# The fifth product of three regions, made of seven quarter products onto PSUM instead of one whole product

## The chip, the cores and the metric

The kernel runs on one core of one Trainium2 chip, as one program. The metric is the device time of one execution in microseconds (us), lower is better. A run is a few executions; the time before is the median of three, 1533.28 us (1532.73 to 1537.7). Engines: PE (TensorE) multiplies, DVE (VectorE) and ACT (ScalarE) add and copy, POOL (GpSimd) and SP (SyncE) start DMAs. Matmul results land in PSUM, which has eight banks (tiles named `ps0` to `ps7` here, 128 x 512 fp32 each). Each engine executes its own queue strictly in the order in which the program wrote it and waits where a semaphore tells it to.

## What is computed

```python
m, k, n = 4096, 4096, 4096
x = np.matmul(a, b)                    # fp32 inputs
return np.where(x > 0, x, alpha * x)   # alpha = 0.01
```

## The kernel before

The output is cut into 16 regions of 1024 x 1024, four groups of rows (g) by four columns (j). Region (0, 0) is a plain blocked product. The other 15 are made one after the other, in the order (0,1), (0,2), (0,3), (1,2), (1,0), (1,3), (1,1), (2,2), (2,0), (2,3), (2,1), (3,2), (3,0), (3,1), (3,3), each by one level of Winograd's form of Strassen's product: A's rows of the group and B's columns are each seen as 2 x 2 blocks (512 x 2048 and 2048 x 512), and seven products of such blocks replace eight. The operands are fp16, sums of blocks are made by DVE. The list PRODUCTS gives the order: a11, a12, s2, s3, s1, a22, s4, each with its block of B (s1 to s4 are sums of blocks of A, the blocks of B are turned into sums in place by `b_sum`). Products one, three, five and seven collect in the four banks `y`, the others in the four banks `z`; a whole product is 64 matmuls of 128 x 128 by 128 x 512 (`product`, L807). Region i + 1 swaps the banks of y and z.

In most regions with g > 0 some products are split a second time in the same way: each block is cut into 2 x 2 quarters, and seven quarter products of 16 matmuls with 256 columns (`quarter_product`, L752) replace the eight that 64 matmuls of 512 columns amount to. Before the change these are the fourth product (`fourth_in_quarters`; not in the first region of a group), the sixth (`sixth_in_quarters`) and the seventh (`seventh_in_quarters`, at the very end `seventh_at_the_end`); the sixth and seventh stay whole in the last region of a group if another group follows (`turning`). In what follows, 4.1 to 4.7, 5.1 to 5.7 and 6.1 to 6.7 are the quarter products of the fourth, fifth and sixth product in the order in which PE gets them.

A product in quarters needs, on the side of A, four sums of quarters. They are made once in a group (`sums_of_a`), kept in DRAM (`kept_q`) and brought back by SP's queue (`load_sums`, L744; for the seventh by ACT's queue) into rooms of the pool `a16`. On the side of B it needs one quarter changed in place (`t3_of_b`, L681) and three sums (`sums_of_b`: sum 2 is L687, sum 4 L689, sum 1 L691), made by DVE in every region into rooms of a tile t. Each is one instruction on 128 x 2048 fp16.

How the order around the change is set: all of it is written by hand (`manual_schedule`); there is no planner. Each engine's queue holds its instructions in the order of the program text below. Tiles in a pool with few buffers bring waits: a new PSUM bank waits until the last reader of the old tile in that bank is done. Semaphores for PSUM go by bank: a DVE add on one half of a bank waits for matmuls into the other half of it, if they stand ahead of it in the text, and the reverse.

In a region such as (2,3), DVE's queue from the fourth product on was: `b_sum` on three blocks (L589); the five adds that take the fourth product's banks into the accumulators v (L1131; the first reads the bank called fourth, the second the one called other); `t3_of_b`, `sums_of_b` (2, 4, 1) for the sixth, `t3_of_b` for the seventh; `add_v` (L978), which adds v into the accumulators u2. These ran beside the fourth and fifth product. Then come the sixth's steps, in `sixth_in_quarters`:

```python
quarter_product(x[0, 0], b[0, 0], into(one), True)      # 6.1
add(v[:2], y[:2]); more(0, 0, one); add(v[2:], y[2:])
quarter_product(sx(1), t(1), into(other), True)         # 6.2
more(1, 1, other)
...                                                     # 6.3
leave(v_pairs, 1, 1)                                    # leaky relu, L313
quarter_product(sx(2), t(2), into(one))                 # 6.4
more(0, 1, one)
...                                                     # 6.5: sx(4), b[1, 1], other
quarter_product(sx(3), b[0, 1], into(one))              # 6.6
```

`add` is L973, `more` is L862. 6.4 writes the bank that the first `more` reads, 6.5 that of the second, 6.6 that of the third. In the last region, (3,3), `judge` tests statistics of the inputs on DVE: three reductions after the fourth product (L621) and, behind `add_v`, a chain of twelve small instructions (L630 to L637).

Of the kernel before, what the change touches and what calls it, by code (L numbers as in the profile page):

```python
# [8 lines left out]
P = 128  # L9
DT = mybir.dt.float16  # L10
# [14 lines left out]
KC = 8  # L25
# [23 lines left out]
def kernel(  # L49
# [610 lines left out]
    kept_s2 = dram_pool.tile([2, P, KC * RM], DT, name="kept_s2")  # L660
    kept_q = {name: dram_pool.tile([4, P, QUARTER], DT, name=f"kept_q{name}") for name in ("a22", "s4")}
    kept_s3 = dram_pool.tile([P, QUARTER], DT, name="kept_s3")
# [29 lines left out]

    def sums_of_a(g, name, room):

        x = {key: q.rearrange("p c m e -> p c (m e)") for key, q in quarters_of_a(g, name).items()}
        made = {}

        def make(n, x0, x1, op):
            made[n] = room(n)
            f = lambda t: made[t].rearrange("p (c m) -> p c m", m=2 * HALF) if isinstance(t, int) else x[t]  # L700
            nc.vector.tensor_tensor(f(n), f(x0), f(x1), op)
            nc.sync.dma_start(kept_q[name][n - 1], made[n])

        make(1, (1, 0), (1, 1), ADD)
        make(2, 1, (0, 0), SUB)
        make(3, (0, 0), (1, 0), SUB)
        make(4, (0, 1), 2, SUB)
# [17 lines left out]
    def sums_of_s3(g, some, room=None):  # L725
# [4 lines left out]
        for n in some:  # L730
# [5 lines left out]
            if n == 4:  # L736
                nc.sync.dma_start(kept_s3, room)

    def s3_rooms(g):
# [43 lines left out]
    for i, (g, j) in enumerate(regions):  # L783
# [64 lines left out]

        def sixth_in_quarters(pairs, banks, v_pairs, v, y, tq, sq):

# [21 lines left out]
            quarter_product(sx(1), t(1), into(other), True)  # L872
            more(1, 1, other)
            following(4)
            next_t[2] = tq[1]
# [7 lines left out]
            quarter_product(sx(4), b[1, 1], into(other))  # L883
            following(1, sq[4])
            next_t[4] = tq[2]
            sums_of_b(y7, next_t, (4,))
            more(0, 1, other)
            quarter_product(sx(3), b[0, 1], into(one))
            following(3)
            more(1, 0, one)  # L890
# [134 lines left out]
        in_quarters = g > 0 and not turning  # L1025
        in_fourth = in_quarters and not first_of_group
        second_of_group = in_fourth and regions[i - 2][0] != g
        early = [measure(i, *block) for block in EARLY.get((g, j), [])]
        for m in early[:1]:
            m.begin()  # L1030
        if first_of_group and g:
            keep_s2(g)

        product(0, y, True)
# [82 lines left out]
        if late_ones:  # L1117
            late_ones[0].end()
        if in_quarters and first_of_group:
            sq = {4: t[:, 3]}  # L1120
            sums_of_a(g, "a22", lambda n: sq.setdefault(n, sq[4] if n == 4 else new_a16()))
            keep_x21(g, "a22")

        z = [new_bank(zbank + mt) for mt in range(MT)]
        if in_fourth or turning and g:
            v_pairs, v, parts = fourth_in_quarters(z, tq, {**s3_rooms(g), 4: a_quarter(sx4)})
            if turning:
                for n in range(3):
                    turn_a_in(0, 1, n)
            for to, bank in parts:  # L1130
                nc.vector.tensor_add(to, bank, to)  # L1131
            if turning:
                add_v()
        else:
            product(3, z, True)
            v_pairs, v = keep(z, side)
        if in_fourth:
            sq = {n: t[:, 3] if n == 4 else new_a16() for n in (1, 2, 3, 4)}
            load_sums("a22", sq, (1, 2, 3, 4))
# [17 lines left out]
        if final:  # L1157
            judged = judge(b_pool.tile([1, P * 6], FP32, name="line", tag="b12"))
            next(judged)
        if in_quarters:  # L1160
            t3_of_b(quarters_of_b(i, 1, 0))
            sums_of_b(quarters_of_b(i, 1, 0), tq)
            t3_of_b(quarters_of_b(i, 1, 1))
            add_v()
            if final:
                good = next(judged)

        product(4, y, False)
        if turning:
            new_s(g + 1, "s1")  # L1170
        if in_quarters:
            tq, sq = sixth_in_quarters(u2_pairs, [new_bank(zbank + mt) for mt in range(MT)], v_pairs, v, y, tq, sq)
        else:
# [6 lines left out]
        if fifth:  # L1180
            fifth = measure(i + 1, *fifth)
            fifth.begin()
            fifth.end()
        fetch_b(i + 1, [(0, 0)], ks)

# [113 lines left out]
```

## Time and profile before

| what | value |
|---|---|
| median of three executions | 1533.28 us (1532.73 to 1537.7) |
| the profiled execution | 1536.2 us, of which its span on the core is 1534.2 us |
| PE busy | 1524.3 us, 99% of the span |
| DVE busy | 1158.9 us, 76% |
| ACT busy | 425.5 us, 28% |
| moved by DMA | 351.26 MB by the queues, mean 229 GB/s |
| region (2,3) on PE | 970.18 to 1062.11 us, 91.93 us |
| its fourth, fifth, sixth, seventh product | from 1011.62, 1023.84, 1037.66, 1049.88 us |

The span runs from the first to the last instruction on the core. In the timeline of an engine each line has the start, the duration, the engine, the line of the kernel, the operation with what it writes and reads, the count of instructions merged into the line, and in brackets the idle time ahead of it and what ended it. Matmuls are pipelined, so the time that one takes is read from start to start, not from the duration. A DVE instruction also overlaps the end of the one ahead of it by some 0.09 us, so DVE too is counted from start to start.

### The profile page before, as it was taken

The page shows a single profiled execution, that of the slowest core. Times are in us where ns is not written, and L with a number is a line of the kernel's source. Part 1 is how long each engine was busy: PE and PEld are TensorE (multiplying, and loading weights), DVE is VectorE, ACT ScalarE, POOL GpSimd, SP SyncE. Part 2 cuts the span into 40 slices and gives each one's busy share as a digit, 9 for nine tenths or more (in the row PEclk, how much of TensorE's full clock was granted, in tenths as well). Part 3 has the DMA queues.
Part 4 walks back from the last instruction along what each step waited for, and adds up shares of the span by engine and source line. Part 5 has one row for each costly group of instructions (what it writes and reads, how often), then busy time and mean ns, then how long its engine had stood idle before and what let it go on. Part 6 is the DMA issues. An engine that isn't in the chain of part 4 may idle for free. (4 is left out here: it accounts for less than half of the span.)

```text
span 1534.2 us, 21785 instructions
## 1 busy us (share of the span) xinstructions
PE 1524.3 (99%) x8667; PEld 847.1 (55%) x8667; DVE 1158.9 (76%) x1207; ACT 425.5 (28%) x730; POOL 258.5 (17%) x426
## 2 busy tenths in 40 slices
PE   9999999999999999999999999999999999999998
PEld 4444444444446567574544747557544475746656
DVE  4368867765699686768769698676976987687677
ACT  2201344646310213103641130312464103041210
POOL 5641110143202011022220001010331100101000
PEclk9999999999999999999999999999999999999999
DMA  9999995998879999899797939669899892948723
GB/s 246 186 215 203 237 281 169 180 197 172 231 277 287 258 278 275 251 289 255 170 288 266 321 148 208 260 157 322 166 241 283 235 349 72 294 162 190 301 97 140
DMA packets 192002, 351.26 MB, mean 229 GB/s; under 512 B 18705, under 2 KB 131601, under 8 KB 178834
## 3 DMA queue, kind: packets, MB, share of 16 engines
q0 software_dynamic: 119808, 112.22, 46.2%
q1 hardware_dynamic: 65458, 211.98, 37.0%
q10 hardware_dynamic: 6624, 25.56, 4.4%
q8 instruction: 70, 1.15, 0.3%
q14 instruction: 42, 0.34, 0.1%
HBM read 344.98 MB, written 114.82 MB: 300 GB/s over the span
## 5 line engine op out<-in xcount | busy, mean ns | idle before, releaser
L807 PE MATMUL ps<-b,a 128*128 128x512 f16 x2624 | 571.1, 379 | 0.5 <-DMA b<-in_b_dram 0.3
L807 PE MATMUL ps<-b,s 128*128 128x512 f16 x2240 | 489.2, 379 | 0.0
L807 PEld LDWEIGHTS <-a 128*128 128x128 f16 x2624 | 256.7, 98 | 308.8 <-issue 1.5
L807 PEld LDWEIGHTS <-s 128*128 128x128 f16 x2240 | 219.1, 98 | 262.5 <-issue 0.4
L589 DVE TENSOR_TENSOR b<-b 128x4096 f16<-128x4096 f16 x104 | 234.6, 2286 | 42.7 <-DMA b<-in_b_dram 34.1
L533 POOL DMA_DIRECT2D b<-in_b_dram x128 | 94.9, 746 | 860.1 <-PE ps L752 437.2
L820 ACT COPY c<-ps 128x512 f32<-128x512 f32 x164 | 84.8, 596 | 469.1 <-PE ps L807 433.3
L142 DVE STREAM_TRANSPOSE a<-a 128x512 uint32<-128x512 uint32 (+2 forms) x120 | 127.0, 1106 | 100.8 <-DMA a<-in_a_dram 100.8
L133 POOL DMA_DIRECT2D a<-in_a_dram x252 | 137.6, 554 | 266.8 <-ACT junk L608 98.2
L608 ACT ACTIVATE junk<-a 128x512 bf16<-128x512 f16 x192 | 121.1, 631 | 99.1 <-DMA a<-in_a_dram 93.8
L752 PEld LDWEIGHTS <-q 128*128 128x128 f16 x1424 | 139.3, 98 | 16.7 <-issue 0.6
L313 DVE SCALAR_TENSOR_TENSOR c<-c 128x1024 f32<-128x1024 f32 (+2 forms) x123 | 141.5, 1190 | 3.8 <-ACT c L820 3.5
L973 DVE TENSOR_TENSOR c<-ps,c 128x512 f32<-128x512 f32 x140 | 87.5, 682 | 55.5 <-PE ps L807 41.8
L231 ACT ACTIVATE sq<-b 128x2048 bf16<-128x2048 f16 x64 | 118.3, 1910 | 37.1 <-DVE sq L240 29.4
L752 PEld LDWEIGHTS <-a 128*128 128x128 f16 x1200 | 117.4, 98 | 18.0 <-issue 0.4
L283 PE MATMUL ps<-b,a 128*128 128x512 f16 x512 | 112.4, 379 | 0.6 <-DVE part L324 0.2
L752 PE MATMUL ps<-b,q 128*128 128x256 f16 x784 | 92.0, 273 | 0.4 <-DVE c L862 0.4
L752 PE MATMUL ps<-b,a 128*128 128x256 f16 x752 | 88.3, 273 | 0.0
L283 PEld LDWEIGHTS <-a 128*128 128x128 f16 x512 | 49.7, 98 | 61.2 <-issue 2.1
L909 ACT COPY c<-ps 128x512 f32<-128x512 f32 x9 | 5.3, 586 | 269.7 <-PE ps L752 148.3
L752 PEld LDWEIGHTS <-s 128*128 128x128 f16 x624 | 61.0, 98 | 7.1
L862 DVE TENSOR_TENSOR c<-ps,c 128x512 f32<-128x512 f32 x80 | 52.2, 683 | 14.4 <-PE ps L752 14.4
(104 smaller groups left out, 904.8 us busy)
## 6 DMA issues: line engine op xcount, KB each, us to landing
b<-in_b_dram POOLq DMA_DIRECT2D x136, 512.0 KB, 11.7
out_dram<-c SPq DMA_DIRECT2D x240, 256.0 KB, 6.3
a<-in_a_dram POOLq DMA_DIRECT2D x244, 128.0 KB, 5.8
b<-kept_half SPq DMA_DIRECT2D x28, 1024.0 KB, 10.9
b<-kept SPq DMA_DIRECT2D x20, 1024.0 KB, 9.2
q<-kept_qs ACTq DMA_DIRECT2D x40, 512.0 KB, 7.8
s<-kept_s SPq DMA_DIRECT2D x18, 1024.0 KB, 7.7
q<-kept_qa SPq DMA_DIRECT2D x28, 512.0 KB, 7.3
```

Of the source, the lines that this page charges most:

```text
L133: nc.gpsimd.dma_start(a16[32 * q:32 * q + 32], src.rearrange("(g i) w -> i g w", i=32))
L142: nc.vector.transpose(part.rearrange("p c m e -> p c (m e)").bitcast(U32) .rearrange("p c (g i) -> p g c i", i=32), src[:, :, i * n:(i + 1 ...
L231: nc.scalar.activation(to, self.parts[n], SQUARE)
L283: nc.tensor.matmul(ps, a_cols(at[0, h, u], c, mt, (h, u) == (0, 0)), bt[0, u, nt][:, c, :], start=first, stop=last,)
L313: nc.vector.scalar_tensor_tensor(t, t, alpha, t, op0=MULT, op1=MAX if alpha <= 1 else MIN)
L533: nc.gpsimd.dma_start(t[:, c:c + 4, :], b_rows(j, u, c, 4, nt, g > 0))
L589: nc.vector.tensor_tensor(f(to), f(x0), f(x1), op)
L608: nc.scalar.activation(junk, piece[:, q, :], SQUARE, accum_out=to[:, 4 * n + q:4 * n + q + 1])
L752: nc.tensor.matmul(to[m], xq[:, c // 2, rows, c % 2], yq[:, c, :], start=first and c == 0 and m < banks, stop=c == KC - 1, skip_group_chec ...
L807: nc.tensor.matmul(banks[mt], a_cols(t, c, mt, t is first_a), B(half, nt, k)[:, c, :], start=first and (k, c) == todo[0], stop=(k, c) == t ...
L820: nc.scalar.copy(kept[mt], banks[mt])
L973: nc.vector.tensor_add(to, bank, to)
```

## The change

In the regions (2,3), (3,1) and (3,3) (the set FIFTH) the fifth product (s1 by a block of B) is made by the new `fifth_in_quarters`: seven quarter products. 5.2, 5.3 and 5.5 add straight onto quarters of the banks y. The other four go into two spare banks of z, `one` and `other`; ACT copies each of these from PSUM into a room in SBUF, and DVE adds the room onto the quarters of y that share it, in PSUM (L876 and L897 of the changed kernel). The rooms lie in the quarter of a22 that the later quarter products don't read; what lay there (a sum of quarters of s3, also used by the fourth product) is kept in DRAM as `kept_s31` and brought back in the next region.

Four sums of quarters of s1 are made in (2,0) and (3,0), on DVE beside their fourth product, and kept in DRAM; each region of FIFTH loads them for its fifth product, and the sums of a22 for its sixth only then. On the side of B, `t3_of_b` and `sums_of_b` for the fifth product come ahead of the fourth's five adds on DVE (sum 1 between the second and the third). `add_v` moves to directly behind these adds. The work for the sixth and seventh product that stood beside the whole fifth product is dealt out: `t3_of_b` and sums 2 and 1 between the steps of the fifth; sum 4 and the seventh's `t3_of_b` in the sixth, behind its second `more` and ahead of `leave`. In (3,3) the chain of `judge` moves behind the fifth product's steps. The fetch of the next region's first block of B takes its halves in the other order.

```diff
@@ sums_of_a @@
-    def sums_of_a(g, name, room):
+    def sums_of_a(g, name, room, some=(1, 2, 3, 4), made=None):
 ...
@@ sums_of_s3 @@
             if n == 4:
                 nc.sync.dma_start(kept_s3, room)
+            if n == 1 and g > 1:
+                nc.sync.dma_start(by_chunk(kept_s31), sx[1])
 ...
+        def fifth_in_quarters(y, one, other, tq, sq, between):
+            b = quarters_of_b(i, 0, 0)
+            x = quarters_of_a(g, "s1")
+            t = lambda n: b_quarter(tq[n])
+            sx = lambda n: a_quarter(sq[n])
+            onto = lambda r, n: [y[2 * r + m][:, n * HALF:(n + 1) * HALF] for m in range(2)]
+            rooms = by_chunk(x21(g, "a22")).bitcast(FP32)
+            rooms = [rooms[:, :2], rooms[:, 2:]]
+
+            def copied(bank):
+                rooms.append(rooms.pop(0))
+                nc.scalar.copy(rooms[1], pair(bank))
+                return rooms[1]
+
+            def more(r, n, room):
+                for m, to in enumerate(onto(r, n)):
+                    nc.vector.tensor_add(to, to, room[:, m])
+
+            quarter_product(x[0, 0], b[0, 0], into(one), True)
+            room = copied(one)
+            quarter_product(sx(4), b[1, 1], onto(0, 1))
+            more(0, 0, room)
+            next(between)
+            quarter_product(x[1, 1], t(4), onto(1, 0))
+            quarter_product(sx(2), t(2), into(one))
+            room = copied(one)
+            quarter_product(x[0, 1], b[1, 0], onto(0, 0))
+            more(0, 1, room)
+            next(between)
+            quarter_product(sx(1), t(1), into(other), True)
+            room = copied(other)
+            more(0, 1, room)
+            more(1, 1, room)
+            quarter_product(sx(3), b[0, 1], into(one))
+            room = copied(one)
+            for m in range(2):
+                to = pair(y[2 + m])
+                nc.vector.tensor_add(to, to, room[:, m].unsqueeze(1).to_broadcast([P, 2, HALF]))
@@ sixth_in_quarters @@
             quarter_product(sx(1), t(1), into(other), True)
             more(1, 1, other)
+            if between:
+                next(between)
             following(4)
 ...
             quarter_product(sx(4), b[1, 1], into(other))
-            following(1, sq[4])
+            following(1, None if between else sq[4])
 ...
             quarter_product(sx(3), b[0, 1], into(one))
-            following(3)
+            following(3, sq[3] if between else None)
@@ the loop over the regions @@
+        if i and regions[i - 1] in FIFTH:
+            for c in range(KC // 2):
+                nc.sync.dma_start(by_chunk(x21(g, "a22"))[:, c], by_chunk(kept_s31)[:, c])
 ...
+        s1_sums = {}
+        if s1_here:
+            sums_of_a(g, "s1", lambda n: t[:, n - 1], (1, 2, 3), s1_sums)
+        if in_fifth:
+            t5 = {2: t[:, 0], 4: t[:, 1], 1: t[:, 2]}
+            t3_of_b(quarters_of_b(i, 0, 0))
+            sums_of_b(quarters_of_b(i, 0, 0), t5, (2, 4))
 ...
-            for to, bank in parts:
+            for n, (to, bank) in enumerate(parts):
+                if in_fifth and n == 2:
+                    sums_of_b(quarters_of_b(i, 0, 0), t5, (1,))
                 nc.vector.tensor_add(to, bank, to)
-            if turning:
+            if turning or in_fifth:
                 add_v()
 ...
+        if s1_here:
+            sums_of_a(g, "s1", lambda n: t[:, 3], (4,), s1_sums)
+        if in_fifth:
+            s5 = {n: t[:, 3] if n == 3 else new_a16() for n in (4, 2, 1, 3)}
+            load_sums("s1", s5, (4, 2, 1, 3))
+        elif in_fourth:
 ...
+        def for_the_sixth():
+            y6 = quarters_of_b(i, 1, 0)
+            t3_of_b(y6)
+            yield
+            sums_of_b(y6, tq, (2, 1))
+            yield
+            sums_of_b(y6, tq, (4,))
+            t3_of_b(quarters_of_b(i, 1, 1))
+            yield
 ...
+        if in_fifth:
+            fifth_in_quarters(y, new_bank(zbank + 3), new_bank(zbank + 1), t5, s5, between)
+            sq = {n: t[:, 3] if n == 3 else new_a16() for n in (1, 2, 4, 3)}
+            load_sums("a22", sq, (1, 2, 4, 3))
             if final:
                 good = next(judged)
-
-        product(4, y, False)
+        else:
+            product(4, y, False)
 ...
-        fetch_b(i + 1, [(0, 0)], ks)
+        fetch_b(i + 1, [(0, 0)], (1, 0) if in_fifth else ks)
```

## The prediction

> **What bounds the kernel now.** I read the page's parts 1 and 2 first, then PE's timeline, then who kept PE waiting, then DVE's timeline beside the products that the change touches.
>
> ```profile
> span 1534.2 us, 21785 instructions
> PE 1524.3 (99%) x8667; PEld 847.1 (55%) x8667; DVE 1158.9 (76%) x1207; ACT 425.5 (28%) x730; POOL 258.5 (17%) x426
> PEclk9999999999999999999999999999999999999999
> ```
>
> PE is the bound, at full clock. So the change is worth what it takes from PE's queue, less each wait that it puts there. The waits of PE, and PE's rows in region (2,3), products four to seven:
>
> ```profile
> PE ps L752 <- DVE c L862: 0.4, 1, 0.4
> ...
> 1022.10 1.91 PE L752 MATMUL ps<-b,a 128*128 128x256 f16 x16
> 1023.84 13.98 PE L807 MATMUL ps<-b,s 128*128 128x512 f16 x64
> 1037.66 1.91 PE L752 MATMUL ps<-b,a 128*128 128x256 f16 x16
> ...
> 1049.88 3.66 PE L752 MATMUL ps<-b,s 128*128 128x256 f16 x32
> ```
>
> A whole product takes 1037.66 - 1023.84 = 13.82 us, seven quarter products 1049.88 - 1037.66 = 12.22 us, 1.747 us each. PE stands still there at no time. DVE in the same place:
>
> ```profile
> 1019.57 0.69 DVE L1131 TENSOR_TENSOR c<-ps,c 128x512 f32<-128x512 f32 x1
> 1021.17 0.69 DVE L1131 TENSOR_TENSOR c<-ps,c 128x512 f32<-128x512 f32 x1 [0.92 <-ACT c L840]
> 1022.91 0.69 DVE L1131 TENSOR_TENSOR c<-ps,c 128x512 f32<-128x512 f32 x1 [1.05 <-ACT c L842]
> 1024.04 1.29 DVE L1131 TENSOR_TENSOR c<-ps,c 128x512 f32<-128x512 f32 x2 [0.44 <-PE ps L752]
> 1025.25 1.21 DVE L681 TENSOR_TENSOR b<-b 128x2048 f16<-128x2048 f16 x1
> 1026.50 1.23 DVE L687 TENSOR_TENSOR q<-b 128x2048 f16<-128x2048 f16 x1
> ...
> 1037.21 1.29 DVE L973 TENSOR_TENSOR c<-ps,c 128x512 f32<-128x512 f32 x2 [3.69 <-PE ps L807]
> 1039.60 0.69 DVE L862 TENSOR_TENSOR c<-ps,c 128x512 f32<-128x512 f32 x1 [1.11 <-PE ps L752]
> ...
> 1042.01 2.35 DVE L313 SCALAR_TENSOR_TENSOR c<-c 128x1024 f32<-128x1024 f32 x2
> 1044.84 0.69 DVE L862 TENSOR_TENSOR c<-ps,c 128x512 f32<-128x512 f32 x1 [0.49 <-PE ps L752]
> ```
>
> From the fourth product's adds to the sixth's third `more` (1044.84) DVE idles only 0.92 + 1.05 + 0.44 + 3.69 + 1.11 + 0.49 = 7.7 us. What happens when it is late there, region (1,2) shows: the third `more`, directly behind L313, ends at 489.41, and 6.6, due at 487.10 + 1.75 = 488.85, starts at 489.46.
>
> ```profile
> 487.10 1.91 PE L752 MATMUL ps<-b,q 128*128 128x256 f16 x16
> 489.46 1.91 PE L752 MATMUL ps<-b,q 128*128 128x256 f16 x16 [0.45 <-DVE c L862]
> ...
> 486.46 2.35 DVE L313 SCALAR_TENSOR_TENSOR c<-c 128x1024 f32<-128x1024 f32 x2
> 488.73 0.68 DVE L862 TENSOR_TENSOR c<-ps,c 128x512 f32<-128x512 f32 x1
> ...
> 1519.47 0.74 DVE L938 TENSOR_TENSOR c<-ps,c 128x256 f32<-128x256 f32 x2
> ```
>
> **The change, part by part.** *PE.* 13.82 - 12.22 = 1.59 us less in each of three regions, 4.8 us in all: the most that there is to win, 0.31%.
>
> *Prices on DVE*, start to start: 128 x 2048 fp16 sum 1.14 us (1.26 where it reads what the one ahead wrote), 128 x 512 add from PSUM 0.605 (four rows of L862 in 2.48), L313 and L978 2.27 a pair. The adds back into PSUM (eight of 128 x 256, two of 128 x 512 a region) are in no row of before. Nearest is L938, 128 x 256 from PSUM into SBUF: two end in 0.74, so 0.33 each; I take that, and 0.605 for the wide ones. Lower end: nothing (an added instruction gives no gain). Upper end: double, 0.69 and 1.21.
>
> [...]
>
> *The queue of DVE in (2,3), moved along.* New ahead of the first L1131: `t3_of_b` and sums 2 and 4, each reading the one before, 3 x 1.25 = 3.76, so it starts at 1023.33 and ends at 1024.03. It frees the bank into which 5.1 goes, due at 1023.84: PE starts at 1024.08, **0.24 late**. Then one add, sum 1, three adds, `add_v` (0.605 + 1.14 + 1.82 + 2.27): 1029.77. First pair of adds into PSUM: 1030.43, in time for 5.5 at 1031.06 (0.6 to spare). `t3_of_b`: 1031.57. The next pair stands behind 5.5 (same banks), which ends at 1032.81; with 0.2 from PE to DVE it runs to 1033.67: here DVE idles 1.4 us although it is behind. Sums 2 and 1: 1036.07. Four adds: 1037.39. Two wide ones: 1038.60 (their copy by ACT is there at 1037.14). The fifth product ends at 1024.08 + 12.23 = 1036.31.
>
> Sixth: two L973, `more`, two L973, `more` (2 x 1.82): 1042.23; 6.4 and 6.5, due at 1041.55 and 1043.30, are served (first `more` 1040.41). Then, new and ahead of `leave`: sum 4 and the seventh's `t3_of_b`, 2.28, then L313 2.27: 1046.78. Only now the third `more`, whose end at 1047.47 releases 6.6 at 1047.52. 6.6 was due at 1036.31 + 5 x 1.747 = 1045.04: **2.49 late** (0.01 from rounding). Region: -1.59 + 0.24 + 2.49 = **+1.14**. Region (3,1) has the same rows at the same distances (b_sum ends 7.95 us after its fourth product starts in both): **+1.14**.
>
> *(3,3)* is the same but for `judge`: its chain ran beside the fifth product from 1499.08 to 1502.27, now 3.25 us stand between the fifth's last adds and the sixth's first. Its three reductions (0.27) fall into the 1.4 us idle. First `more` 3.25 later: 6.4 waits 2.26, 6.5 another 0.07, 6.6 another 3.41: -1.59 + 0.24 + 5.74 = **+4.39**.
>
> *The seventh product* then starts as late as the sixth ended; DVE leaves the sixth about 5 us after that start (4.3 before) and has 6.42 us idle later there, so the lateness dies in it.
>
> *ACT.* Four copies of 0.59 a region; it idled from 1022.9 to 1053.6 apart from four DMA issues. 5.4 needs the copy of 5.1, done 0.83 after 5.1's end, 2.7 ahead of 5.4. Nothing, as long as ACT is free within these 2.7 us; beyond, 5.4 would be late by the rest.
>
> *(2,0) and (3,0).* Four sums of s1, 4.7 us of DVE, against 3.69 idle ahead of L973 at 945.27 and 1.1 in smaller gaps: nothing on PE. On SP the store of the fourth sum now stands ahead of the four loads for the sixth: in (2,0) they leave at about 937.3 and not at 925.16. 6.2 (947.5) is 10 us away; loads of `kept_qa` land in 3.1 to 8.7. The last load waits for that store too (stores of such sums: median 2.6 to 7.0): 937.3 + 7.0 + 8.7 = 953.0 against 6.5 at 952.7, so 0 to 0.3; I take 0.
>
> *Other DMAs in the three regions.* The loads for the fifth leave where the sixth's did (1017.05, then every 1.75); even at 8.7 they land at 1025.8, 1027.5, 1029.2, 1031.0, needed at 1025.8, 1029.3, 1032.8, 1034.6. The sixth's leave as 5.2, 5.4, 5.6, 5.7 end: at 8.7 they land at 1036.3, 1039.8, 1043.3, 1045.0, needed at 1038.1, 1041.6, 1043.3, 1045.0. No wait, but no room. SP stands with the last of these until 5.7 ends; behind it are only the stores of `leave`, due 10 us later. POOL's fetches of the next region's first block start within 2 us of before and are needed 25 us later. The reload of `kept_s31` queues on SP at the next region's start, 41 us ahead of its reader. In all some 11 MB more beside 351.
>
> *Sum.* 1.14 + 1.14 + 4.39 = **+6.7 us**. The profiled execution (1536.2 us, span 1534.2, 2.0 outside it) lies 2.9 above the median, so I add to the median: 1533.3 + 6.7 = **1540.0**. With adds into PSUM for nothing the sum is +2.3 (1535.6), at the double price +17.7 (1551.0).
>
> **Rivals.** *DVE keeps up* and PE's 1.59 come through: 1533.3 - 4.8 = 1528.5. For it: DVE is busy only 76%. It decides if the third `more` of the sixth ends 2.5 us earlier than I have it, 5.7 in (3,3); against it, even adds for nothing give 1.5.
>
> *DVE is less late*: at 0.2 us for a quarter add and 0.4 for a wide one, two thirds of the rows, the sum is 4.7 us, and below that it is inside 4.6 (0.3%, about what a measurement of this kernel can tell from no change): 1537. Against it, L938, timed in this kernel on the same form of input.
>
> *Loads late.* If the sixth's loads take 11.7 us, as POOL's fetches of B do in the median, 6.5 waits 3.0 in (2,3) and (3,1), in the place of 6.6's 2.49, and in (2,0) up to 3.3: about +11, 1544.
>
> *The clock.* The first eleven matmuls of the trace take 4.87 us, 0.44 each where 0.216 is the rule later: after PE's rest they ran at half speed. If the 3.4 us pause in (3,3) brings that back for some 4 us, 2 us are lost: 1542. No later pause of before is over 0.45 us, so no row tells.
>
> [...]
>
> **How the numbers follow.** My forecast 0.70, DVE less late 0.12, DVE keeps up 0.07, loads late 0.07, clock 0.04. Slower by over 0.3%: 0.70 + 0.07 + 0.04 = 0.81; within: 0.12; faster: 0.07. The range is that of the unknown price, 1535.6 to 1551.0; it holds the late loads and the clock, and leaves out DVE keeping up.
>
> **What would show it.** In (2,3) and (3,1) PE idles about 2.3 us (the 0.61 late in (1,2) show as 0.45) ahead of 6.6 <- DVE `more`, with L313 directly ahead of it on DVE; in (3,3) two pauses, about 2 and 3 us; seven quarters in 12.2 us in the fifth; adds into PSUM 0.33 start to start. Wrong, if 6.6 starts on time in (2,3), or if PE's waits name DMAs.

## The result, and the profile after

The changed kernel takes 1548.36 us (median of six executions, 1545.8 to 1551.28), the kernel before 1533.57 beside it (six, 1532.73 to 1537.7): ratio 1.0091, 95% interval 1.0074 to 1.0108. It is slower by 14.8 us where +6.7 was forecast. The direction was right, and the time lies inside the range, but the size was off by more than a factor of two. Two later measurements of the same kernel on other chips gave 1.0074 (1.0061 to 1.0087) and 1.0084 (1.0066 to 1.0103), +11.8 and +13.8 us.

The head of the page of the changed kernel, profiled in an execution of 1549.76 us:

```profile
span 1547.6 us, 22192 instructions
PE 1522.6 (98%) x8811; PEld 861.4 (56%) x8811; DVE 1192.7 (77%) x1257; ACT 432.3 (28%) x742; POOL 258.2 (17%) x426
```

PE has 144 matmuls more (three regions, each 112 of 256 columns for 64 of 512) and is busy 1.7 us less and not 4.8, because some matmuls ran at half clock (2.69 us, below). Its span is 13.4 us longer: the rest went into waits. Who kept PE waiting:

```profile
PE ps L759 <- DVE c L912: 11.0, 5, 3.2
PE ps L814 <- DMA b<-in_b_dram: 4.2, 2, 3.4
...
PE ps L759 <- DVE c L1198: 0.9, 1, 0.9
...
PE ps L814 <- DVE b L589: 0.2, 1, 0.2
```

L912 is `more` of the sixth product (L862 before), L1198 one of the fourth's five adds (L1131 before), L814 a whole product (L807 before). The first line is what the prediction spoke of; the second is the one that it said must not be there; of its 4.2 us, 3.4 stand in (1,0), some 370 us ahead of the first transfer that the change adds. PE's timeline in (2,3), from 4.7 over 5.1 to 6.6:

```profile
1027.86 1.91 PE L759 MATMUL ps<-b,a 128*128 128x256 f16 x16
1029.84 1.91 PE L759 MATMUL ps<-b,s 128*128 128x256 f16 x16
...
1042.07 1.91 PE L759 MATMUL ps<-b,a 128*128 128x256 f16 x16
...
1049.06 1.91 PE L759 MATMUL ps<-b,q 128*128 128x256 f16 x16
1053.19 1.91 PE L759 MATMUL ps<-b,q 128*128 128x256 f16 x16 [2.23 <-DVE c L912]
```

The fifth product takes 1042.07 - 1029.84 = 12.23 us, as forecast. 5.1 is 1029.84 - 1027.86 - 1.747 = 0.23 late, 6.6 is 1053.19 - 1049.06 - 1.747 = 2.38 late. DVE over the same stretch:

```profile
1035.50 0.76 DVE L876 TENSOR_TENSOR ps<-ps,a 128x256 f32<-128x256 f32 x2
1036.16 1.22 DVE L683 TENSOR_TENSOR b<-b 128x2048 f16<-128x2048 f16 x1
1038.74 0.77 DVE L876 TENSOR_TENSOR ps<-ps,a 128x256 f32<-128x256 f32 x2 [1.35 <-PE ps L759]
...
1041.80 1.42 DVE L876 TENSOR_TENSOR ps<-ps,a 128x256 f32<-128x256 f32 x4
1043.13 1.29 DVE L897 TENSOR_TENSOR ps<-ps,a 128x512 f32<-128x512 f32 x2
1044.32 1.28 DVE L1025 TENSOR_TENSOR c<-ps,c 128x512 f32<-128x512 f32 x2
...
1047.91 1.22 DVE L691 TENSOR_TENSOR q<-b,q 128x2048 f16<-128x2048 f16 x1
1049.04 1.23 DVE L683 TENSOR_TENSOR b<-b 128x2048 f16<-128x2048 f16 x1
1050.17 2.37 DVE L313 SCALAR_TENSOR_TENSOR c<-c 128x1024 f32<-128x1024 f32 x2
1052.44 0.70 DVE L912 TENSOR_TENSOR c<-ps,c 128x512 f32<-128x512 f32 x1
```

Four L876 from 1041.80 to 1043.13 are 0.33 each, two L897 from 1043.13 to 1044.32 are 0.60 each. DVE idles 1.35 us ahead of the second pair, where 1.4 was forecast. The third `more` (1052.44) stands behind sum 4, `t3_of_b` and L313, and PE starts 6.6 0.05 us behind its end.

In (3,3) PE waits three times and not twice (6.4, 6.6, and the second half of 7.1):

```profile
1517.96 1.91 PE L759 MATMUL ps<-q,q 128*128 128x256 f16 x16 [1.88 <-DVE c L912]
...
1524.88 1.91 PE L759 MATMUL ps<-b,q 128*128 128x256 f16 x16 [3.23 <-DVE c L912]
...
1528.37 0.27 PE L759 MATMUL ps<-b,s 128*128 128x256 f16 x1
1530.14 3.54 PE L759 MATMUL ps<-b,s 128*128 128x256 f16 x31 [1.49 <-DVE c L912]
```

To account for the rest I count, for each matmul, by how much it starts later than its columns allow at full clock (0.216 us per 512 columns, 0.109 per 256), and add these delays up by place, leaving out the first 100 us, which are alike. The three profiles of the changed kernel are a (this one), b and c (the two later ones):

| delay of PE, us | forecast | a | b | c |
|---|---|---|---|---|
| 5.1 in the three regions, order on DVE | 0.72 | 0.72 | 0.72 | 0.72 |
| 6.6 in (2,3) and (3,1) | 4.98 | 4.77 | 4.77 | 4.76 |
| 6.4, 6.5 and 6.6 in (3,3) | 5.74 | 5.43 | 5.43 | 5.45 |
| second half of 7.1 in (3,3) | 0 | 1.66 | 0.84 | 0.84 |
| start of (3,1) on a late block of B, and what follows there | 0 | 2.12 | 2.20 | 2.46 |
| (2,0), loads of a22's sums | 0 | 0 | 0 | 1.13 |
| matmuls at half clock | 0 | 2.69 | 4.10 | 4.10 |
| waits at other places | 0 | 4.01 | 3.55 | 0.77 |
| sum | 11.44 | 21.40 | 21.61 | 20.23 |

Taken off are 4.77 us of matmuls saved; the kernel before has 2.07 of such delays in its own profile. For a that leaves 14.6 us; its last matmul starts 1542.14 - 1527.36 = 14.8 us later than before's. (In the span it is 1.3 less, because the stretch from the last matmul's start to the end took 6.8 us in before's profile and 5.5 in a.) Not all of that lies behind the change: in a, the 2.69 us of half clock and 3.58 of the waits at other places stand in (1,0), at 507 to 516 us, 6.3 us together. In b and c the half clock lies directly behind waits ahead of 6.6.

So the first three rows, the mechanism forecast, came out at 6.2 us net where 6.7 was predicted. The other rows, which the prediction had at nothing, are larger: 9.3 to 10.7 us, of which the kernel before has 2.07 as well.

### The profile page after: what moved, and what is told of

The parts are those of the page before. It is cut to its first block, busy times and chain, and to the rows that moved or that the text cites. A ratio compares the mean times of both kernels' runs of the same rounds, so it can differ in the third digit from the quotient of the medians.

```text
span 1547.6 us, 22192 instructions
## 1 busy us (share of the span) xinstructions
PE 1522.6 (98%) x8811; PEld 861.4 (56%) x8811; DVE 1192.7 (77%) x1257; ACT 432.3 (28%) x742; POOL 258.2 (17%) x426
## 5 line engine op out<-in xcount | busy, mean ns | idle before, releaser
L814 PE MATMUL ps<-b,a 128*128 128x512 f16 x2624 | 573.7, 381 | 4.2 <-DMA b<-in_b_dram 4.2
L814 PE MATMUL ps<-b,s 128*128 128x512 f16 x2048 | 447.3, 379 | 0.2 <-DVE b L589 0.2
L814 PEld LDWEIGHTS <-a 128*128 128x128 f16 x2624 | 257.4, 98 | 314.4 <-issue 8.6
L814 PEld LDWEIGHTS <-s 128*128 128x128 f16 x2048 | 200.3, 98 | 240.9 <-issue 1.0
L759 PEld LDWEIGHTS <-q 128*128 128x128 f16 x1616 | 158.1, 98 | 28.7 <-issue 10.4
L313 DVE SCALAR_TENSOR_TENSOR c<-c 128x1024 f32<-128x1024 f32 (+2 forms) x123 | 141.8, 1195 | 3.8 <-ACT c L827 3.6
L1025 DVE TENSOR_TENSOR c<-ps,c 128x512 f32<-128x512 f32 x140 | 87.6, 684 | 39.4 <-PE ps L814 25.8
L759 PE MATMUL ps<-b,q 128*128 128x256 f16 x880 | 103.9, 273 | 7.7 <-DVE c L912 7.7
L759 PEld LDWEIGHTS <-s 128*128 128x128 f16 x768 | 75.1, 98 | 11.9 <-issue 3.3
L759 PE MATMUL ps<-q,q 128*128 128x256 f16 x624 | 74.0, 273 | 1.9 <-DVE c L912 1.9
## 6 DMA issues: line engine op xcount, KB each, us to landing
b<-in_b_dram POOLq DMA_DIRECT2D x136, 512.0 KB, 13.4
```

Source lines behind the costliest of these rows:

```text
L313: nc.vector.scalar_tensor_tensor(t, t, alpha, t, op0=MULT, op1=MAX if alpha <= 1 else MIN)
L759: nc.tensor.matmul(to[m], xq[:, c // 2, rows, c % 2], yq[:, c, :], start=first and c == 0 and m < banks, stop=c == KC - 1, skip_group_chec ...
L814: nc.tensor.matmul(banks[mt], a_cols(t, c, mt, t is first_a), B(half, nt, k)[:, c, :], start=first and (k, c) == todo[0], stop=(k, c) == t ...
```

## The experiments

My theory, once the result was there: the order on DVE gives what was forecast, and the transfers, which were costed at nothing, give the rest, as waits for blocks of B. The rivals: the order costs all of it in some way that I had missed; or PE's clock falls after the pauses; or the waits on transfers come by chance, whatever the kernel.

### One region, and none

In the kernel with one region alone, only (2,3) has its fifth product in quarters:

```diff
-    FIFTH = {(2, 3), (3, 1), (3, 3)}
+    FIFTH = {(2, 3)}
-        s1_here = (g, j) == (2, 0) or (g, j) == (3, 0)
+        s1_here = (g, j) == (2, 0)
```

> Only (2,3) makes its fifth product in quarters; the sums of s1 are made and kept in (2,0) alone. Theory A (the waits of PE come from the order of DVE's queue): -1.59 + 0.24 + 2.39 = +1.0 us over the kernel before, 1534.6, with waits of 0.24 ahead of 5.1 and 2.4 ahead of 6.6. Theory B (a part comes from something that the changed program brings everywhere, its layout in DRAM or its size, and that shows as the 3.6 us wait for B at the start of (1,0)): +1.0 and another 4 to 6, 1539. In both, the late B at the start of (3,1) should be gone if the stores and loads of (3,0) cause it.

Measured: 1537.69 us, ratio 1.0025 (1.0014 to 1.0037), +2.8 us. The profile, of the quickest of its twelve executions (1535.42), has 0.24 ahead of 5.1 and 2.39 ahead of 6.6, and 0.64 in (2,0). The net of (2,3), +1.04, is where the forecast had it; with (2,0) it is 1.7. What the median has beyond that, no profile shows.

With no region at all, but the sums of s1 made and stored, and the quarter of s3 stored:

```diff
-    FIFTH = {(2, 3), (3, 1), (3, 3)}
+    FIFTH = set()
```

> No region makes its fifth product in quarters, but the sums of s1 are still made and stored in (2,0) and (3,0), and the sum of s3 is kept. Theory A: within 0.5 us of the kernel before, 1533.6. Theory C (the stores of the sums, and the four loads that queue behind the last of them, make B late for (3,1)): a wait of about 1 us at the start of (3,1) and about 1 more by DVE there, +1 to +2, 1535. Theory B: +4 to +6, with a wait of over 3 us at the start of (1,0).

Measured: 1536.19 us, ratio 1.0007 (0.9998 to 1.0016): at most 2.5 us. Its profile shows one wait of 0.86 in (2,0), for a sum of a22 that the store on SP's queue holds up. That is the place which the prediction had at "0 to 0.3; I take 0".

### The order on DVE, mended

The sixth's third `more` ahead of sum 4, the seventh's `t3_of_b` and `leave`:

```diff
             more(1, 1, other)
-            if between:
-                next(between)
             following(4)
 ...
-            leave(v_pairs, 1, 1)
+            if not between:
+                leave(v_pairs, 1, 1)
 ...
             more(0, 1, one)
+            if between:
+                next(between)
+                leave(v_pairs, 1, 1)
```

> The changed kernel, but DVE does the sixth's third add (the one that releases 6.6) ahead of sum 4, of the seventh's change in place and of the leaky relu, not behind them. Theory A: the 2.4 us ahead of 6.6 go in (2,3) and (3,1); in (3,3) DVE is busy without a break, so the wait only moves from 6.6 to the seventh's first matmuls, which need the sixth's last add: 1548.4 - 4.8 = 1543.6. Theory C (loads): 6.6 stays late, no change.

Measured: 1546.7 us, ratio 1.0081 (1.0067 to 1.0095). The waits ahead of 6.6 in (2,3) and (3,1) are gone, as intended; the time, at +11.8 us, is not told from that of the whole change. Its profile is of the quickest of its six executions (1542.07). PE's timeline, in (2,3) and in (3,3):

```profile
1056.17 3.65 PE L759 MATMUL ps<-q,q 128*128 128x256 f16 x32 [0.51 <-ACT c L963]
...
1517.22 0.28 PE L759 MATMUL ps<-b,s 128*128 128x256 f16 x1 [1.77 <-DVE c L912]
1520.74 5.21 PE L759 MATMUL ps<-b,s 128*128 128x256 f16 x31 [3.24 <-DVE c L912]
```

In (2,3) 0.24 + 0.67 us, in the seventh product, stand in the place of 2.39, a saving of 1.5; in (3,1) it is 1.2. But in (3,3) the 3.39 us ahead of 6.6 and the 1.66 of 7.1 become 1.93 + 3.41, all at 7.1. DVE had the same work to do by the time when the seventh product needed its banks, so there the delay is paid one product later. That is the backlog, not the place of one instruction. The 31 quarter matmuls behind the long pause take 5.21 us and not 3.54: by that duration half of them ran at half clock (mean granted clock of the profile: 0.998).

Four mends together: that one, the fourth's first add ahead of the fifth's sum 4, the chain of `judge` ahead of the third product, and for the seventh at the end the other spare bank as its second:

```diff
+        if final:
+            judged = judge(c_pool.tile([1, P * 6], FP32, name="line", tag=f"c{1 - side}"))
+            next(judged)
 ...
-            sums_of_b(quarters_of_b(i, 0, 0), t5, (2, 4))
+            sums_of_b(quarters_of_b(i, 0, 0), t5, (2,))
 ...
+                if in_fifth and n == 1:
+                    sums_of_b(quarters_of_b(i, 0, 0), t5, (4,))
 ...
-            rest = y, new_bank(zbank + 3), new_bank(zbank + 2), tq, sq
+            spare = (1, 2) if in_fifth and final else (2, 1)
+            rest = y, new_bank(zbank + 3), new_bank(zbank + spare[0]), tq, sq
```

> As third_more_first, and three more edits to the order: the fourth product's first add ahead of sum 4 of the fifth (for 5.1), the chain of judge in (3,3) ahead of the third product, and in (3,3) the seventh takes as its first bank the one that the sixth's 6.5 used, not that of 6.7. Theory A: no wait of PE on DVE is left in the three regions, so 1533.6 - 4.8 = 1528.8, and up to 2 more if B stays late for (3,1): 1529 to 1531. Theory B: 4 to 6 above that, 1534. The change as such costing PE time beyond the order (adds into PSUM, copies): above 1536.

Measured: 1541.98 us, ratio 1.005 (1.0036 to 1.0063), +7.0 us, the least of the kernels that make the whole product with all three regions, and still slower than before. In its profile 5.1, 6.4, 6.5 and 6.6 are on time or nearly so, but the seventh product is 0.9 us late in (2,3) and 1.2 in (3,1), 7.1 still waits 1.98 + 1.62 in (3,3), and (2,1) brought a new wait. DVE and PE there:

```profile
1088.70 2.10 DVE L142 STREAM_TRANSPOSE a<-a 128x512 uint32<-128x512 uint32 x2 [4.17 <-DMA a<-in_a_dram]
```

```profile
1101.51 3.66 PE L759 MATMUL ps<-b,a 128*128 128x256 f16 x32
1108.04 3.54 PE L759 MATMUL ps<-q,a 128*128 128x256 f16 x16 [2.87 <-DVE q L691]
1111.37 1.99 PE L759 MATMUL ps<-q,s 128*128 128x256 f16 x16
```

DVE had waited 4.17 us for blocks of A, so the sums for the fourth product of (2,1) came 3 us late; and the product behind that pause (3.54 us for 16 quarter matmuls, 1.91 elsewhere) ran at half clock (mean granted clock of the profile: 0.997).

### The order without the transfers, and the transfers without the order

To part the two, on one chip: the whole change once more; the order alone (the sums of s1 made and not stored, the fifth product with a22's sums, which the sixth uses again; the quarter of s3 still moves); and the transfers alone (the fifth product whole as before, with the sums of s1 that the stores need).

> The changed kernel as it is, a second time. If the 3.6 us wait for B at the start of (1,0), far ahead of the change, belongs to the program, it is in this profile again; if it is chance, it is not, and the waits that stay are those in and behind the three regions: 0.24 and 2.4 in (2,3) and (3,1), 0.24, 2.0, 3.4 and 1.7 in (3,3), which with 4.77 saved give +7.8 us, and what is over that up to about +14 lies in waits for loads that change from run to run.

```diff
-            nc.sync.dma_start(kept_q[name][n - 1], made[n])
+            if name != "s1":
+                nc.sync.dma_start(kept_q[name][n - 1], made[n])
 ...
-            load_sums("s1", s5, (4, 2, 1, 3))
+            load_sums("a22", s5, (4, 2, 1, 3))
 ...
-            sq = {n: t[:, 3] if n == 3 else new_a16() for n in (1, 2, 4, 3)}
-            load_sums("a22", sq, (1, 2, 4, 3))
+            sq = s5
```

> The changed kernel with its order on DVE, ACT and PE, but without most of its new transfers: the sums of s1 are not stored, and the fifth takes the sums of a22 in their place, which the sixth then uses again without a second load (so the fifth product of three regions is wrong). Only the 0.5 MB of kept_s31 still move. Theory A (the order on DVE is all): +7.8 and no less, and if transfers play no part the same as the changed kernel on this chip. Theory C (the rest over +7.8 comes from the new transfers): +7.8, that is 5 to 7 us faster than the changed kernel.

```diff
-        in_fifth = (g, j) in FIFTH
+        in_fifth = False
+        dmas_of_fifth = (g, j) in FIFTH
 ...
+            if dmas_of_fifth:
+                sq = {n: t[:, 3] if n == 4 else new_a16() for n in (1, 2, 3, 4)}
+                load_sums("s1", sq, (1, 2, 3, 4))
 ...
+            if dmas_of_fifth:
+                load_sums("a22", sq, (1, 2, 3, 4))
             product(4, y, False)
```

> The other half: the fifth product whole as before, DVE's order as before, but all new transfers are made (stores of the sums of s1 in (2,0) and (3,0) with the DVE sums, loads of them in the three regions, then the loads of a22's sums, and kept_s31 out and back). Theory A: within 1 us of the kernel before. Theory C: +3 to +6 us over it, in waits for B, for the sums or for A, in (2,0), (2,1), (3,1).

Measured: the whole 1.0074 (1.0061 to 1.0087), +11.8 us; the order alone 1.0062 (1.0049 to 1.0075), +9.1; the transfers alone 1.0026 (1.0012 to 1.0039), +4.5. The profile of the order alone has no wait for a block of B left. It has the forecast's 6.2 us net, 1.66 ahead of the second half of 7.1, and 1.5 of half clock: 9.4, against 2.1 to 2.8 that the kernel before loses in its own waits. The order, then, is most of the loss. The transfers seem to take some part, though the intervals of the whole and of the order alone overlap.

But which? The profile of the transfers alone has its largest wait in (1,0), some 370 us ahead of the first transfer that the change adds:

```profile
509.54 5.72 PE L814 MATMUL ps<-b,a 128*128 128x512 f16 x18 [2.08 <-DMA b<-in_b_dram]
```

### The kernel before, and the transfers one by one

The kernel before, measured a second time as a control:

> The kernel before once more, as a control and for a second profile of it. If the waits of PE for blocks of B from DRAM (2.24 us at the start of (1,0) with the transfers added alone, 3.58 with the whole change) belong to the added transfers, its profile shows none over 0.5 us behind the first 100 us, and the ratio is 1.000 with both ends within 0.001. If they come by chance whatever the kernel, one of 1 to 4 us may stand in its profile as well, and its executions scatter as far as those of the kernel with the transfers alone (8.6 us from lowest to highest).

Measured: ratio 0.9997 (0.9986 to 1.0008). PE's row in (1,0), and then two lines from the list of what kept PE waiting:

```profile
506.51 8.79 PE L807 MATMUL ps<-b,a 128*128 128x512 f16 x40 [0.18 <-DMA b<-in_b_dram]
```

```profile
PE ps L807 <- ACT c L820: 1.1, 1, 1.1
...
PE ps L807 <- DMA b<-in_b_dram: 0.2, 1, 0.2
```

The same wait is there in the kernel before (0.31 in its first profile, 0.18 here), and none or below 0.2 in the profiles of most others. It comes and goes; so does another of 1.1 us, for ACT, at 1171. It was long (1.0 to 3.4) only in profiles of kernels with more transfers, but it stands ahead of all of them; why, stays open.

Then a22's sums loaded twice in the three regions, and the quarter of s3 kept and reloaded:

```diff
             load_sums("a22", sq, (1, 2, 3, 4))
+            if (g, j) in FIFTH:
+                load_sums("a22", sq, (1, 2, 3, 4))
```

> The kernel before, but the four sums of a22 are loaded twice, the second time straight behind the first, in (2,3), (3,1) and (3,3): twelve more loads of 0.5 MB, 6.3 of the 12.6 MB that the change adds. The stores of the sums of s1 alone cost 0.07%. If the volume of loads behind the fourth product is what costs 4.5 us in the kernel with the transfers alone, this takes most of it: +3 to +4.5 us (1.0020 to 1.0030). If it is the reload of one quarter at the next region's start, or the scatter of the runs, +0 to +1 us (1.0000 to 1.0007).

```diff
+            if n == 1 and g > 1:
+                nc.sync.dma_start(by_chunk(kept_s31), sx[1])
 ...
+        if i and regions[i - 1] in FIFTH:
+            for c in range(KC // 2):
+                nc.sync.dma_start(by_chunk(x21(g, "a22"))[:, c], by_chunk(kept_s31)[:, c])
```

> The kernel before, with only the quarter of s3 kept in DRAM and brought back at the start of the region behind (2,3) and (3,1): two stores and two times two loads, some 2 MB. If these loads stand in the way on SP's queue at the start of the region, +2 to +4.5 us, with a wait in (2,1) or (3,3). If the loads for the fifth product cost, +0 to +1 us (1.0000 to 1.0007).

Measured: 1.0001 (0.9991 to 1.0011) and 1.0001 (0.9992 to 1.0009). Neither is a price. Of my expectation, the branch by which the volume of loads costs 3 to 4.5 us is refuted.

On the same chip, the change without its ten adds into PSUM:

```diff
-                for m, to in enumerate(onto(r, n)):
-                    nc.vector.tensor_add(to, to, room[:, m])
+                pass
 ...
-                to = pair(y[2 + m])
-                nc.vector.tensor_add(to, to, room[:, m].unsqueeze(1).to_broadcast([P, 2, HALF]))
+                pass
```

> The changed kernel without the ten adds into PSUM of each of the three regions (so the fifth product lacks four of its quarter products there). By the prediction's prices the adds are worth 4.4 us in the sum (+6.7 with them, +2.3 without), since DVE then reaches the sixth earlier: 6.6 is some 1.4 us less late in each region. If the time behind the change is the order on DVE, the ratio falls by 0.003 from that of the whole change (1.0074 to 1.0091), to 1.0045 to 1.0060, and the wait ahead of 6.6 in (2,3) is about 1.0 us where it was 2.4. If the adds in PSUM disturb PE itself, more than that goes.

Measured: 1.0038 (1.0024 to 1.0051), +5.7 us. 6.6 in (2,3), PE's timeline:

```profile
1044.54 1.91 PE L759 MATMUL ps<-b,q 128*128 128x256 f16 x16 [0.72 <-DVE c L910]
```

It is 0.89 late where it was 2.38; in (3,3) 6.4 is on time and 6.6 1.55 late. The adds are worth 1.5 us in (2,3) and in (3,1), 3.9 in (3,3), 6.9 in all, more than the 4.4 by which the forecast differed with the adds for nothing. In (2,3) DVE now has no backlog at all (it idles 3.44 us ahead of the sixth's first `more`), and yet 6.6 is late: sum 4, `t3_of_b` and L313 between the second and the third `more` are enough for that. Even so the change doesn't pay: 5.7 us remain, 2.9 of them at (3,1) and 2.8 in (2,1) by the profile.

### Which transfers: the stores

The blocks of B for (3,1) are fetched by POOL's queue in the last 58 us of (3,0). Their landing, by the DMA view of that stretch (issues, KB each, median us from issue to landing), in the kernel before:

```profile
b<-in_b_dram POOLq DMA_DIRECT2D x8, 512.0 KB, 8.6
```

and in the changed kernel, where four stores of the sums of s1 stand in the same stretch:

```profile
b<-in_b_dram POOLq DMA_DIRECT2D x8, 512.0 KB, 17.0
...
kept_qs<-q SPq DMA_DIRECT2D x4, 512.0 KB, 8.4
```

The bytes moved there are the same (16.0 and 16.1 MB), but the fetches take twice as long. How busy the DMA engines are in that stretch, in tenths by 40 slices, before and changed:

```profile
DMA  0002999999999999999999999999999999999999
...
DMA  0000699999999999999999999999999999999999
```

The engines had next to no room in either, so what the stores move there something else must give up. The blocks of `kept_half`, which SP's queue fetches, also take 13.9 us in place of 10.1. By the landing of the fetches of B there, all kernels up to here fall into two groups: 8.6 to 10.5 us in the six that have no stores in (3,0), 16.1 to 17.4 in the seven that have them. What a late block does to (3,1) in the changed kernel, on PE and on ACT:

```profile
1359.05 19.15 PE L814 MATMUL ps<-b,a 128*128 128x512 f16 x88 [0.79 <-DMA b<-in_b_dram]
1378.36 13.97 PE L814 MATMUL ps<-b,s 128*128 128x512 f16 x64 [0.16 <-DVE b L589]
...
1405.49 1.91 PE L759 MATMUL ps<-b,s 128*128 128x256 f16 x16 [0.93 <-DVE c L1198]
```

```profile
1359.09 1.91 ACT L231 ACTIVATE sq<-b 128x2048 bf16<-128x2048 f16 x1 [2.94 <-DMA b<-in_b_dram]
```

PE starts 0.95 late, and ACT idles 2.94 us for that block, of which it makes squares. DVE's statistics and `b_sum` wait for them, so a whole product starts another 0.32 late, and DVE brings the rest of its lateness to 5.1: 1.09 where 0.24 came from the order. That is 2.12 us in all.

To test it, on a fourth chip: the whole change without these stores (and the fifth product made with a22's sums, loaded in their own right), the whole change with the stores and without the second set of loads, and the whole.

```diff
-            nc.sync.dma_start(kept_q[name][n - 1], made[n])
+            if name != "s1":
+                nc.sync.dma_start(kept_q[name][n - 1], made[n])
 ...
-            load_sums("s1", s5, (4, 2, 1, 3))
+            load_sums("a22", s5, (4, 2, 1, 3))
```

> The whole change, but the sums of s1 are made and not stored, and the fifth product of the three regions is made with the sums of a22 in their place (so its result there is wrong); the eight loads of a region, the reload and the order of all engines stay. In the profiles so far the blocks of B for (3,1) take 16 to 17 us to land where the four stores of (3,0) are there, and 9 to 11 where they are not; of the four profiles of the changed fifth product in which they took 17 or more, all show PE late at the start of (3,1) by 0.9 to 2.0 us, and behind it 5.1 late by up to 0.85 more than the order on DVE alone makes it. If these stores are the price, the landing falls to 9 to 11 us, (3,1) starts on time, 5.1 is 0.24 late there, and the time is 2 to 3 us under that of the whole change. If the twelve added loads are the price, it is within 1 us of the whole change.

```diff
-            load_sums("s1", s5, (4, 2, 1, 3))
+            load_sums("a22", s5, (4, 2, 1, 3))
 ...
-            sq = {n: t[:, 3] if n == 3 else new_a16() for n in (1, 2, 4, 3)}
-            load_sums("a22", sq, (1, 2, 4, 3))
+            sq = s5
```

> The whole change, with the four stores of the sums of s1 in (2,0) and (3,0), but the fifth product made with the sums of a22, which the sixth uses again (so the fifth product's result is wrong in the three regions): twelve loads less than the whole change. If the stores are the price, the blocks of B take 16 to 17 us to land ahead of (3,1), and the time is within 1 us of the whole change. If the loads are, it is that of the order alone, 1.0062 (1.0049 to 1.0075), some 2 to 3 us under the whole change.

> The whole change once more, beside the two kernels that leave out a part of its transfers, on the same chip: 1.0074 to 1.0091, and 1.6 to 4 us of lost clock in some of its executions, which show as a granted clock of 0.996 to 0.998.

Measured: 1.0064 (1.0045 to 1.0084) without the stores, 1.0075 (1.0058 to 1.0092) without the second loads, 1.0084 (1.0066 to 1.0103) for the whole. In the median the stores are worth 3.1 us and the loads 2.0, and by the intervals alone neither is told from nothing. The profiles tell them apart. The DMA view of the kernel without the stores, in the same stretch:

```profile
b<-in_b_dram POOLq DMA_DIRECT2D x8, 512.0 KB, 9.4
```

(3,1) then starts on time and 5.1 is 0.24 late; the 2.1 to 2.5 us are gone. Without the second loads the fetches take 17.4 us, and the same 0.93 + 0.32 + 0.85 are there as in the whole.

The transfers alone, measured again on this chip:

> The transfers added and the fifth product whole, once more on another chip: +4.5 us (1.0026) if the transfers cost by themselves. If the first look at it was long by waits that come by chance, +1 to +1.5 us (1.0007 to 1.0010), the sum of the parts measured one by one (stores 1.0007, loads 1.0001, reload 1.0001).

Measured: 1.0012 (0.9998 to 1.0027), +2.3 us, within what its parts gave one by one; its executions lie from 1533.4 to 1542.1. So the first measurement's +4.5 did not come again; the two intervals overlap, and chance may be the difference. Neither of its profiles has a wait at the start of (3,1): the fetches took 16.6 and 16.4 us there. The ten profiles with the stores in (3,0) lie on two sides of an edge: at 16.1 to 16.6 us (four of them) the block is just in time, at 17.0 to 17.4 (six, the three of the changed kernel among them) it is 0.6 to 1.7 us late. Why the whole change lies beyond the edge and the transfers alone don't, the runs don't show.

### The clock

The windows of the third profile of the changed kernel (start and end, us, busy time and count of PE, weight loads, DVE, ACT and POOL, then the granted clock, the DMA share and GB/s):

```profile
1495.00:1514.00 19.00, 17.63 (x160) 15.65 (x160) 17.63 (x38) 2.34 (x4) 0.00 (x0) 1.00 0.48 164
1521.40:1527.00 5.60, 5.55 (x27) 3.83 (x27) 4.75 (x6) 0.00 (x0) 0.00 (x0) 0.50 0.63 226
1530.00:1538.00 8.00, 8.00 (x76) 7.18 (x74) 5.38 (x9) 1.85 (x6) 0.00 (x0) 1.00 0.37 135
```

The second stretch lies directly behind the pause ahead of 6.6 in (3,3): the granted clock is 0.50, and 26 quarter matmuls take twice their time, 2.6 us lost. (0.8 of it would have been spent waiting for 7.1's bank anyway, which is why that row is 0.84 in b and c.) In the first profile of the changed kernel the same pause, of the same 3.39 us, left the clock at full:

```profile
1525.00:1530.00 5.00, 3.64 (x33) 3.12 (x32) 5.00 (x7) 0.00 (x0) 0.00 (x0) 1.00 0.79 286
```

The 2.38 us ahead of 6.6 in the other two regions went both ways as well. In a the granted clock stayed at 1.00 behind the pause in (2,3) (from 1053 to 1058 us); in b it was 0.57 in the mean behind the same pause (1050 to 1054), and in c 0.62 behind the one in (3,1) (1423.7 to 1428).

Over all profiles after the first 100 us, half clock came behind 7 of 14 pauses of 2.2 to 2.4 us, behind 6 of 11 pauses of 2.7 to 3.6, and behind one pair of 1.98 and 1.62 us close together; behind no other pause of 1.5 to 2.1 (15 of them). Each time it cost 1.5 to 2.7 us. So the length of a pause alone does not tell the two outcomes apart: 13 of the 25 from 2.2 to 3.6 us had half clock behind them.

The whole executions agree. The quickest of the changed kernel's second measurement, 1543.34 us, had a mean granted clock of 1.000 and is 9.2 us over before's median there; the longest, 1549.35, had 0.996.

## Why the prediction was low

The mechanism forecast is there, and at its size: 6.2 us net for 6.7. What failed are three steps that the sum put at nothing: the fall of the clock (4.1 us in b and c), the stores beside POOL's fetches in (3,0) (2.1 to 2.5), and the seventh product's second bank (0.8 to 1.7). In a the clock's part came elsewhere, behind a wait in (1,0), ahead of the change; that one stays open.

*PE's saving and the prices on DVE* were right. Seven quarters took 12.23 us; a quarter add into PSUM took 0.33 and a wide one 0.60, what L938 and L862 had given.

*The queue of DVE, moved along* was right to 0.2 us in (2,3) and to 0.4 in (3,3): 0.23 and 2.38 for 0.24 and 2.49; 2.04 and 3.39 for 2.26 and 3.41. The order alone, measured as a kernel, costs 9.1 us, and its profile puts 6.2 net on these waits.

*"The lateness dies in it"*, of the seventh product, failed: 7.1 waits 0.84 to 1.66 for its second bank in (3,3). The step looked at how long DVE needs, and not at which bank the seventh takes. The sixth now uses its banks in the order 0, 2, 1, 3, so the second bank of 7.1 is the one that the sixth's very last add reads. The wait names it (DVE c L912). In the mended kernels, where that bank is swapped or the third add is early, the wait grows: DVE's backlog is what is late next, and it doesn't die within the sixth product.

*"(2,0) and (3,0) ... nothing on PE"* failed too. It followed SP's queue and the loads behind the stores, and there it took the low end: 0.6 to 1.2 us came in (2,0) in five of the eleven profiles with these stores. In (3,0) it left out that the four stores move in the same stretch as POOL's fetches of B for the next region, on DMA engines that were busy already. The fetches' landing went from 9 to 17 us, and the block came 0.95 us late, 2.1 us with what follows. The prediction weighed POOL's fetches only in the three regions of the change, as "needed 25 us later".

*The clock* was listed as a rival at 0.04, tied to the 3.4 us pause in (3,3) and priced at 2 us. The price was near for one pause (2.6), the condition wrong: half clock came behind pauses of 2.2 to 2.4 us as well (7 of 14), and the change makes three pauses above 2.2. So 4.1 us came in b and c, more than any other step that failed. The mistake was to make it a rival of the forecast, when it rides on top of it: the forecast itself had pauses of 2.5 and 3.4 us, and half clock came behind 13 of the 25 pauses of 2.2 to 3.6. Which of them it comes behind, their length alone does not settle: the 3.39 us in (3,3) had 0.50 behind them in c and 1.00 in a.

*Loads late* was the rival at 0.07. In the three regions none of the sixth's loads was late; in (2,0) they were, by up to 1.2 us in the profiles named above. The transfer that PE's waits name in a is of another queue.

*The range* held the time by luck, for the wrong reason. Its upper end stood for adds at double the price, and the adds cost what was taken.

What stays open is the run of waits "at other places": 0.8 to 4 us in the three profiles, among them (1,0), ahead of the change, and (2,1), where 4.3 was 2.7 to 3.0 us late in three of the other kernels, the three of all 17 profiles in which DVE waited 3.8 to 4.2 us for blocks of A ahead of it (1.6 at most in the others). The kernel before has 2.1 and 2.8 us of delays of its own in its two profiles. That they are chance fits the spread of the executions; no run shows what makes them long.

No kernel here beat the one before. Nothing in the runs points to one: the order costs more than the 4.8 us to be won even without its transfers, and mending it moves the delay to the seventh product.

## What to carry to other kernels

When work is dealt to an engine that is on time only because it idles a little between steps, follow the backlog until an idle stretch truly takes it up. Where it is mended in one place it turns up at the next thing that waits for that engine, and a change in the order of buffers decides which that is. Price an added transfer not only by who waits for it but by what shares the engines in that stretch, and look at the slack of those transfers. And a forecast that puts pauses of over 2 us on PE should carry the price of a fall of the clock with a chance of its own, on top of the pauses; here half clock came behind 13 of 25 such pauses of 2.2 to 3.6 us, at 1.5 to 2.7 us each.

## What the runs showed that I had not expected

- Half clock came behind 7 of 14 pauses of PE of 2.2 to 2.4 us and behind 6 of 11 of 2.7 to 3.6. The same pause of 3.39 us had a granted clock of 0.50 behind it in c and of 1.00 in a. Half clock cost 1.5 to 2.7 us each time, about as much as the pause.
- Four stores of 512 KB from SP's queue in (3,0) brought the fetches of 512 KB on POOL's queue from 9 to 17 us, at the same bytes in the same stretch of time.
- Twelve loads more of 512 KB on SP's queue cost nothing that could be measured (1.0001, 0.9991 to 1.0011).
- DVE adds in place in PSUM with an operand from SBUF took what adds from PSUM into SBUF took: 0.33 us for 128 x 256, 0.60 for 128 x 512, start to start.
